# Instruction order in four stages of a decoder layer: start, retention, convolution, passage to the feed-forward part

## The chip, the cores and the metric

The kernel runs on one core of a Trainium2 chip. A core has TensorE (PE, matmul), VectorE (DVE), ScalarE (ACT), GpSimd (POOL) and queues that issue transfers (SyncE, SP, most of them); each engine works through its own queue in order. The metric is device time of one execution in microseconds, the median of the runs.

## The reference

One decoder layer on x of 2048 x 1024 float32, batch 1. A vector c gives shift, scale and gate for two sub-layers (adaLN). The mixing sub-layer puts h = x (1 + scale) + shift through one input projection; its columns feed a gated short convolution and a retention with four heads in chunks of 128. Both results are put through one output projection, then comes a layer norm of alpha x + gate * mix, and then a SwiGLU feed-forward part of width 2816 with a second norm.

```python
mod = sc @ ada_w[layer] + ada_b[layer]
h = x * (1.0 + scale_m) + shift_m
mix = _hybrid_mixer(h, w_in[layer], conv_w[layer], w_out[layer])
x = _layernorm(DN_ALPHA * x + gate_m * mix, ln1_g[layer], ln1_b[layer])
h = x * (1.0 + scale_f) + shift_f
ff = _swiglu(h, w_gate[layer], w_up[layer], w_down[layer])
x = _layernorm(DN_ALPHA * x + gate_f * ff, ln2_g[layer], ln2_b[layer])
...
scores = jnp.einsum('bnihd,bnjhd->bhnij', qc, kc) * decay_mask[None, :, None]
intra = jnp.einsum('bhnij,bnjhe->bnihe', scores, vc)
...
y_conv = _short_conv_mixer(cg, xin, bg, conv_w)
```

## The kernel before

**Numbers.** A float32 matrix is scaled by a power of two from its largest absolute value and split into a high and a low float16 part. A product takes three matmuls (mm3, lines 135 to 137: high x high, high x low, low x high). The high part is made by ScalarE (line 130, or a plain copy), the low part by VectorE (line 131, or a subtraction). The convolution's and the feed-forward's products use seven products in place of eight, with sums and differences of the blocks ahead of and behind them: differences of weights (S1 to S4) and of inputs (T1 to T4), and sums of results (p1, u2, e5). Each of the seven is 4 x 3 = 12 matmuls of 128x512.

**Memory.** Tiles of 128x2048 float32 are "pages" (pg), 24 in all, which are freed and taken by hand. Results of TensorE lie in two pools of four banks, "mm" and "ax", which rotate: the fifth product of a pool waits until the first one's bank has been read.

**Order.** The kernel is written as one sequence of calls. At build time a scheduler with a timeline simulation turns it into one queue for each engine; the order of calls and marks such as `tc.issue_after(x)` (the instructions in the block stand behind x, on x's engine) decide what it may do.

**Stages.** *Start*: input rows, first weights and adaLN sums; `start_bound` bounds the largest h (lines 286, 87, 291), `ret_half_max` takes a weight maximum (line 87). *Retention*, sixteen tiles t of 128 rows: `gemm_ret(t, u)` makes q, k, v and the gate (u = 0 to 3, 24 matmuls each) and evicts them (lines 705 by VectorE, 709 and 711 by ScalarE); `rotary` (734 to 736), `ret_scores` with its masking on VectorE (767), `ret_kv` (782), and for the tile before `ret_y` (793, 796), its norm (800 to 810) and its splits. In between `ret_h(p)` and `ret_hsplit(p)` modulate the rows of a later pair of tiles (line 296, ScalarE) and split them; `h_again` does so once more for the convolution's input. *Convolution*, twelve units: `conv_pair(u, b)` for u = 0 to 5 and both halves b of the sequence, with the seven products in the order 0, 5, 4, 1, 6, 3, 2. `cw_split(u)` scales a unit's weights (880), makes their differences on GpSimd (881 to 884) and both parts of all of them (888 ScalarE, 889 VectorE). `ada_sum` (199) sums modulation weights as they arrive. *Output projection*: pairs of tiles j in the order 0, 1, 4, 5, 6, 7, 2, 3, counted by i. `op_half(t, g)` adds one half of the projection to y (1307), `norm1` is the norm (1267 to 1278, its scaling 1278 by ScalarE), `h2_pair(j)` makes the feed-forward input and its differences (1341 to 1355), `h2_turn(j)` transposes it by transfers (1374). *Passage*: with i = 7 the first feed-forward weights are split: `gu_split1(q)` A11, A12, S1, A22 (1412, 1413), `gu_split2(q)` S2 to S4 (1421 to 1423 the differences, 1426, 1427 the parts). `gu(q, bl)` is one block of the feed-forward's first half for half bl of the sequence. Then come 22 weight blocks q, and the second half. The blocks from about 935 us on are the same before and after.

In `gu` the order of the products and of the sums that free their banks stands as written:

```python
prod(pa, "A11", B11, True, True)
nc.scalar.activation(p1, pa, AF.Copy)
prod(pb, "S2", T2, True, True)
...
prod(pc, "S1", T1_, True, True)
...
prod(pa, "A12", B21, False, True)
...
prod(pd, "A22", T4, True, True)
```

Of the kernel before, what the change touches and what calls it, by code (L numbers as in the profile page):

```python
# [11 lines left out]
F16 = mybir.dt.float16  # L12
# [28 lines left out]
def kernel(ctx: ExitStack, tc: tile.TileContext, xT, x, c, adaN, adaT, ada_b, w_ret, w_conv,  # L41
                             conv_w, w_out, ln1, ln1c, w_gu, w_dn, ln2, rope, consts, out):
    nc = tc.nc
# [531 lines left out]
    with in_order():  # L575
# [75 lines left out]
        ret_half_max(0, 1)  # L651
        start_bound(1, 0)
        start_bound(1, 1)
        start_all(2, 0, (1,))
# [34 lines left out]
    T1 = {}  # L689

    def gemm_ret(t, u):
# [16 lines left out]
        elif u != 3:  # L708
            nc.scalar.activation(dst, ps, AF.Copy, scale=iv)
        else:  # L710
            nc.scalar.activation(dst, ps, AF.Silu, scale=iv)
# [158 lines left out]

    def cw_split(u):
# [12 lines left out]
        nc.gpsimd.tensor_sub(sv[:, 2], f[:, 2], sv[:, 1])  # L884
        cw_views(u)
# [64 lines left out]
    def conv_pair(u, b, done=lambda m: None):  # L950
# [24 lines left out]
        nc.scalar.activation(e5, pc, AF.Copy, scale=iv)  # L975
        prod(pa, 1, False, True)
        prod(pb, 6, False, True)
        nc.vector.scalar_tensor_tensor(p1, pb, iv, p1, op0=OP.mult, op1=OP.add)
        nc.gpsimd.tensor_add(e5, e5, p1)
        pd = new()  # L980
        prod(pd, 3, True, True)
# [94 lines left out]
    for t in range(4, NT):  # L1076
# [22 lines left out]
        if end:  # L1099
            free(*ret_pages[2:4])  # L1100
            cw_split(0)
            cw_max(1)
            hp_load(0, 0)
            hp_load(0, 5)
# [13 lines left out]
        if end:  # L1118
# [3 lines left out]
            hp_load(0, 6)  # L1122
        if t % 2 == 0 and p < 8:
            ret_h(p)
            ret_hsplit(p)
# [3 lines left out]
        if end:  # L1129
            free(*ret_pages[6:8])  # L1130
            hp_load(0, 3)
# [3 lines left out]
        if t in AGAIN:  # L1135
            h_again(AGAIN.index(t))
        elif chores:
            chores.pop()()
# [32 lines left out]
    ahead = [0, 5, 4, 1, 6, 3, 2]  # L1171
    for b in range(2):
        for u in range(6):
# [41 lines left out]
            conv_pair(u, b, done)  # L1215
# [58 lines left out]
    def norm1(y):  # L1274
# [3 lines left out]
        nc.scalar.activation(y, y, AF.Identity, scale=rs, bias=nm)  # L1278
# [50 lines left out]
    def h2_pair(j, tp=None):  # L1329
# [4 lines left out]
        fp = yp[j] if tp else page()  # L1334
# [8 lines left out]
        if tp:  # L1343
            t = [tp[:, i * 512:(i + 1) * 512] for i in range(3)]
# [64 lines left out]
    def gu_split1(q):  # L1409
# [5 lines left out]
        gu_w[q] = {"A11": av[:, :, 0], "A12": av[:, :, 1], "S1": av[:, :, 2], "A22": av[:, :, 3], "pages": [wa]}  # L1415

    def gu_split2(q, eng):
        pg = gu_stage.pop(q)
# [10 lines left out]
        w = gu_w[q]  # L1429
# [8 lines left out]
    u32, ucount, gu_last, gu_pe = [], [0], [None], [None]  # L1438
# [3 lines left out]
    def gu(q, bl, between=None):  # L1442
# [20 lines left out]
        nc.scalar.activation(p1, pa, AF.Copy)  # L1463
        prod(pb, "S2", T2, True, True)
        nc.vector.tensor_add(u2, pb, p1)
# [5 lines left out]
        nc.scalar.activation(u[:, 0], pa, AF.Silu, scale=iv_g)  # L1471
        pd = new()
        prod(pd, "A22", T4, True, True)
        prod(pb, "S3", T3, False, True)
# [4 lines left out]
        prod(pc, "S4", B22, False, True)  # L1479
# [420 lines left out]
```

## Time and profile before

| | us |
|---|---|
| median of 3 runs | 2106.2 (2104.92 to 2108.79) |
| profiled execution | 2106.87 |
| its span | 2104.7 |
| TensorE busy in the span | 2023.1 (96%) |
| VectorE, ScalarE, GpSimd busy | 1463.8, 666.9, 904.9 |
| transfers | 361.06 MB, mean 172 GB/s |

Stage borders on TensorE in us of the span: start to 186, retention to 461, convolution to 790, output projection to 875, passage to 935, then the feed-forward's two halves. The clock is the share of full speed that was granted to TensorE. A row's "idle before" is the time in which the engine stood ahead of the instruction, with the instruction that released it.

### The profile page before, as it was taken

Reading aid. Unit: us, or ns where it says so; the run is one execution under the profiler, and the core shown is the slowest. Engines: PE = TensorE matmul, PEld = TensorE weight load, DVE = VectorE, ACT = ScalarE, POOL = GpSimd, SP = SyncE. Lnnn points to the kernel's source line nnn. Section 1 sums busy time; section 2 is a strip of 40 time slices with the busy share of each in tenths; the row PEclk is TensorE's granted clock in tenths of the full one; section 3 lists DMA queues with packets and bytes.
Section 4 is the critical chain, followed back from the end, with each engine's and each line's share of the span. In section 5 each row is a group of like instructions: output and inputs, shape, how many; then the busy total and the mean of one; then the engine's idle time right before and its main releaser. Section 6 shows DMA issues by size and latency. Waiting matters only on the chain.

```text
span 2104.7 us, 24640 instructions
## 1 busy us (share of the span) xinstructions
PE 2023.1 (96%) x9631; PEld 948.0 (45%) x9631; DVE 1463.8 (70%) x1793; ACT 666.9 (32%) x728; POOL 904.9 (43%) x751
## 2 busy tenths in 40 slices
PE   8899998989899999789999999999999999999998
PEld 3354554444344544334444444444444444444443
DVE  7898846567686577766678768877777354478564
ACT  5523443433422223332323223343433222212210
POOL 3554855555642377742323114544444143134232
PEclk9999999999999999999999999999999999999999
DMA  9048544576873298742444553434343665375321
GB/s 380 26 135 260 163 133 110 161 236 212 269 307 125 85 251 195 186 128 71 149 170 166 184 189 126 160 126 154 131 150 120 237 263 198 139 272 190 150 77 74
DMA packets 189492, 361.06 MB, mean 172 GB/s; under 512 B 118080, under 2 KB 118080, under 8 KB 166592
## 3 DMA queue, kind: packets, MB, share of 16 engines
q1 hardware_dynamic: 181168, 344.55, 49.1%
q10 hardware_dynamic: 8208, 14.95, 2.1%
q8 instruction: 75, 1.23, 0.2%
q14 instruction: 41, 0.34, 0.0%
HBM read 231.26 MB, written 100.93 MB: 158 GB/s over the span
## 4 chain that ended last, share of the span: by engine, by line
PE 42%; DVE 8%; POOL 5%; DMA 5%; issue 2%; ACT 2%; SPq 0%; POOLq 0%; DVEq 0%; ACTq 0%
PE mm L135 7%; PE mm L136 7%; PE mm L137 7%; PE ax L135 7%; PE ax L137 7%; PE ax L136 7%; DMA pg<-yscr 2%; DMA pg<-in_w_dn_dram 2%; POOL pg L1342 1%; DVE pg L1617 1%; ACT pg L1278 1%; DVE wdm L87 1%; DVE pg L1618 1%; DVE pg L1482 1%; POOL rs L1270 1%
## 5 line engine op out<-in xcount | busy, mean ns | idle before, releaser
L135 PE MATMUL mm<-pg,pg 128*128 128x512 f16 x1604 | 609.4, 382 | 18.4 <-ACT pg L1426 8.2
L136 PE MATMUL mm<-pg,pg 128*128 128x512 f16 x1604 | 611.2, 381 | 0.0
L137 PE MATMUL mm<-pg,pg 128*128 128x512 f16 x1604 | 609.5, 381 | 1.7 <-DVE pg L889 1.7
L135 PE MATMUL ax<-pg,pg 128*128 128x512 f16 x1220 | 462.9, 380 | 9.3 <-DVE t2k L973 3.8
L137 PE MATMUL ax<-pg,pg 128*128 128x512 f16 x1220 | 462.6, 380 | 1.5 <-DVE pg L889 1.5
L136 PE MATMUL ax<-pg,pg 128*128 128x512 f16 x1220 | 463.3, 380 | 0.0
L136 PEld LDWEIGHTS <-pg 128*128 128x128 f16 x2888 | 283.3, 98 | 350.4 <-issue 23.7
L135 PEld LDWEIGHTS <-pg 128*128 128x128 f16 x2888 | 283.3, 98 | 345.7 <-issue 9.5
L137 PEld LDWEIGHTS <-pg 128*128 128x128 f16 x2888 | 283.1, 98 | 340.7 <-issue 6.4
L1476 POOL TENSOR_TENSOR pg<-pg,t2k 128x512 f32<-128x512 f32 x44 | 57.9, 1315 | 383.2 <-DVE t2k L1475 207.6
L131 DVE SCALAR_TENSOR_TENSOR pg<-pg,p2s,pg 128x2048 f16<-128x2048 f32 (+1 forms) x42 | 95.9, 2294 | 134.5 <-ACT pg L130 134.4
L130 ACT ACTIVATE pg<-pg,p2s 128x2048 f16<-128x2048 f32 (+1 forms) x42 | 77.6, 1858 | 262.2 <-PE mm L136 114.1
L87 DVE TENSOR_REDUCE m<-pg 128x2 bf16<-128x2048 f32 (+1 forms) x38 | 86.3, 2275 | 20.9 <-DMA pg<-in_w_gu_dram 10.8
L525 PE MATMUL mm<-pg,pg 128*128 128x512 f16 x384 | 89.1, 387 | 5.6 <-DVE pg L533 2.5
L1481 ACT ACTIVATE pg<-t2k,ivg 128x512 f32<-128x512 f32 x44 | 31.6, 717 | 178.1 <-DVE t2k L1480 178.1
L1530 DVE TENSOR_TENSOR pg<-pg,pg 128x2048 f16<-128x2048 f32 (+1 forms) x22 | 46.3, 2103 | 44.6 <-ACT pg L1529 44.6
L1413 DVE TENSOR_TENSOR pg<-pg,pg 128x2048 f16<-128x2048 f32 x22 | 51.7, 2349 | 31.7 <-ACT pg L1412 31.7
L1529 ACT ACTIVATE pg<-pg 128x2048 f16<-128x2048 f32 (+1 forms) x22 | 37.3, 1697 | 99.6 <-DMA wscr<-pg 57.8
L131 DVE SCALAR_TENSOR_TENSOR pg<-pg,hs,pg 128x1024 f16<-128x1024 f32 x32 | 49.4, 1547 | 26.8 <-ACT pg L130 26.6
L1270 POOL TENSOR_SCALAR rs<-mv 128x1 f32<-128x1 f32 x32 | 30.5, 957 | 82.2 <-DVE mv L1268 79.6
L1583 POOL TENSOR_TENSOR pg<-pg,pg 128x2048 f32<-128x2048 f32 (+1 forms) x6 | 26.9, 4491 | 82.0 <-DVE pg L131 38.6
L525 PEld LDWEIGHTS <-pg 128*128 128x128 f16 x384 | 37.5, 99 | 52.4 <-issue 7.7
(278 smaller groups left out, 2782.7 us busy)
## 6 DMA issues: line engine op xcount, KB each, us to landing
pg<-wscr SPq DMA_DIRECT2D x28, 1024.0 KB, 4.8
pg<-in_w_gu_dram SPq DMA_DIRECT2D x22, 1024.0 KB, 4.9
uscr<-pg SPq DMA_DIRECT2D x44, 512.0 KB, 2.8
pg<-in_w_dn_dram SPq DMA_DIRECT2D x22, 1024.0 KB, 5.9
pg<-in_adaT_dram SPq DMA_DIRECT2D x21, 1024.0 KB, 8.2
wscr<-pg SPq DMA_DIRECT2D x77, 256.0 KB, 2.9
yscr<-pg SPq DMA_DIRECT2D x16, 1024.0 KB, 4.3
pg<-uscr SPq DMA_DIRECT2D x16, 1024.0 KB, 5.7
```

The lines of the kernel that those rows point to most:

```text
L87: return nc.vector.tensor_reduce(dst, src, axis=AX.X, op=OP.max, apply_absolute_value=True).ins
L130: nc.scalar.activation(hi, src, AF.Copy, scale=s)
L131: nc.vector.scalar_tensor_tensor(lo, src, s, hi, op0=OP.mult, op1=OP.subtract)
L135: nc.tensor.matmul(ps, l_hi, r_hi, start=start, stop=False, skip_group_check=again)
L136: nc.tensor.matmul(ps, l_hi, r_lo, start=False, stop=False, skip_group_check=again)
L137: return nc.tensor.matmul(ps, l_lo, r_hi, start=False, stop=stop, skip_group_check=again).ins
L525: nc.tensor.matmul(ps, hv[:, a, k, o], w[:, k], start=n == 0 and k == k0, stop=n == 2 and k == k1 - 1)
L1270: nc.gpsimd.tensor_scalar(rs, mv[:, 1:2], EPS / (ALPHA * ALPHA), None, op0=OP.add)
L1413: nc.vector.tensor_sub(wa[:, 2048:], pg, wa[:, :2048])
L1476: nc.gpsimd.tensor_add(e5, e5, p1)
L1529: nc.scalar.activation(o[:, :n, 0], src, AF.Copy)
L1530: nc.vector.tensor_sub(o[:, :n, 1], src, o[:, :n, 0])
```

## The change

- Start: the two bounds of the second pair of rows stand ahead of the weight maximum.
- Retention: `ret_h` and `ret_hsplit` of a later pair are issued behind the ScalarE eviction of u = 2, `h_again` and other small jobs behind that of u = 3. Two loads of the convolution's input change places.
- Convolution: `cw_split` keeps scaling and differences; the parts and their stores are a new function `cw_finish`, called for unit u + 1 in the middle of unit u, behind the eviction of product 4 (e5). Product 3 goes ahead of product 6. 
- Passage: the differences of the first two weight blocks are made on VectorE. With i = 7 both second halves of the projection come first, then `gu_split2(1)`, then the norms, whose scaling is kept back until `gu`'s A12 activation. The first two blocks run `late`: S2 and S4 go behind A22. `gu(0, 1)` stands ahead of `gu_split1(1)`. The last pair's `h2_pair` writes into another page, where before it wrote into y in place behind y's store. Two weight scalings are issued behind a product.

The code, with unchanged lines cut:

```diff
         start_mod(1)
-        ret_half_max(0, 1)
         start_bound(1, 0)
         start_bound(1, 1)
+        ret_half_max(0, 1)
         start_all(2, 0, (1,))
...
     T1 = {}
+    evicted = [None]
...
         elif u != 3:
-            nc.scalar.activation(dst, ps, AF.Copy, scale=iv)
+            evicted[0] = nc.scalar.activation(dst, ps, AF.Copy, scale=iv).ins
         else:
-            nc.scalar.activation(dst, ps, AF.Silu, scale=iv)
+            evicted[0] = nc.scalar.activation(dst, ps, AF.Silu, scale=iv).ins
...
+    cw_parts = {}
...
         nc.gpsimd.tensor_sub(sv[:, 2], f[:, 2], sv[:, 1])
+        cw_parts[u] = (pg, f, sv)
+    def cw_finish(u):
+        pg, f, sv = cw_parts.pop(u)
         cw_views(u)
...
-    def conv_pair(u, b, done=lambda m: None):
+    def conv_pair(u, b, done=lambda m: None, between=None):
         w = cw[u]
...
         prod(pc, 4, True, True)
-        nc.scalar.activation(e5, pc, AF.Copy, scale=iv)
+        read = nc.scalar.activation(e5, pc, AF.Copy, scale=iv).ins
+        if between:
+            with tc.issue_after(read):
+                between()
         prod(pa, 1, False, True)
+        pd = new()
+        prod(pd, 3, True, True)
         prod(pb, 6, False, True)
...
         nc.gpsimd.tensor_add(e5, e5, p1)
-        pd = new()
-        prod(pd, 3, True, True)
         nc.vector.scalar_tensor_tensor(p1, pd, iv, p1, op0=OP.mult, op1=OP.add)
...
             cw_split(0)
+            cw_finish(0)
             cw_max(1)
...
             hp_load(0, 1)
-            hp_load(0, 6)
+            hp_load(0, 3)
         if t % 2 == 0 and p < 8:
-            ret_h(p)
-            ret_hsplit(p)
+            with tc.issue_after(evicted[0]):
+                ret_h(p)
+                ret_hsplit(p)
         if t == NT - 2:
...
             free(*ret_pages[6:8])
-            hp_load(0, 3)
+            hp_load(0, 6)
             hp_load(0, 2)
...
             ret_mix(2)
-        if t in AGAIN:
-            h_again(AGAIN.index(t))
-        elif chores:
-            chores.pop()()
+        with tc.issue_after(evicted[0]):
+            if t in AGAIN:
+                h_again(AGAIN.index(t))
+            elif chores:
+                chores.pop()()
         if t % 2 == 1:
...
-    ahead = [0, 5, 4, 1, 6, 3, 2]
+    ahead = [0, 5, 4, 1, 3, 6, 2]
     for b in range(2):
...
                 free(spp)
-            conv_pair(u, b, done)
+            conv_pair(u, b, done, (lambda u=u: cw_finish(u + 1)) if n < 5 else None)
             if n == 0:
...
         nc.gpsimd.tensor_scalar(nm, mean, rs, -1.0, op0=OP.mult, op1=OP.mult)
-        nc.scalar.activation(y, y, AF.Identity, scale=rs, bias=nm)
+        def scaled():
+            nc.scalar.activation(y, y, AF.Identity, scale=rs, bias=nm)
+        return scaled
...
             hlv.extend(pg.rearrange("p (s a n) -> p s a n", s=4, a=2) for pg in hl)
-        fp = yp[j] if tp else page()
+        fp = tp or page()
         f = fp.rearrange("p (s n) -> p s n", s=4)
...
         if tp:
-            t = [tp[:, i * 512:(i + 1) * 512] for i in range(3)]
+            t = [owner[id(hl[1])][1][:, 1536:2048], yp[j][:, :512], yp[j][:, 512:1024]]
         else:
...
         av = wa.rearrange("p (a s k n) -> p a s k n", a=2, s=4, k=4)
-        gu_w[q] = {"A11": av[:, :, 0], "A12": av[:, :, 1], "S1": av[:, :, 2], "A22": av[:, :, 3], "pages": [wa]}
+        w = gu_w.setdefault(q, {"pages": []})
+        w.update({"A11": av[:, :, 0], "A12": av[:, :, 1], "S1": av[:, :, 2], "A22": av[:, :, 3]})
+        w["pages"].insert(0, wa)
     def gu_split2(q, eng):
-        pg = gu_stage.pop(q)
+        pg = gu_stage[q]
         a = pg.rearrange("p (s n) -> p s n", s=4)
...
         bv = ws[:, :3072].rearrange("p (a s k n) -> p a s k n", a=2, s=3, k=4)
-        w = gu_w[q]
+        w = gu_w.setdefault(q, {"pages": []})
         w.update({"S2": bv[:, :, 0], "S3": bv[:, :, 1], "S4": bv[:, :, 2], "tmp": owner[id(ws)][1][:, 1536:2048]})
...
-    u32, ucount, gu_last, gu_pe = [], [0], [None], [None]
+    u32, ucount, gu_last, gu_pe, gu_act = [], [0], [None], [None], [None, None]
     uscr = [[dram.tile([2, P, NCH, 512], F32, name=f"uscr{b}{r}") for r in range(2)] for b in range(2)]
...
-    def gu(q, bl, between=None):
+    def gu(q, bl, between=None, late=False):
...
         prod(pa, "A11", B11, True, True)
-        nc.scalar.activation(p1, pa, AF.Copy)
-        prod(pb, "S2", T2, True, True)
-        nc.vector.tensor_add(u2, pb, p1)
+        gu_act[0] = nc.scalar.activation(p1, pa, AF.Copy).ins
+        if not late:
+            prod(pb, "S2", T2, True, True)
+            nc.vector.tensor_add(u2, pb, p1)
         prod(pc, "S1", T1_, True, True)
...
         prod(pa, "A12", B21, False, True)
-        nc.scalar.activation(u[:, 0], pa, AF.Silu, scale=iv_g)
+        gu_act[1] = nc.scalar.activation(u[:, 0], pa, AF.Silu, scale=iv_g).ins
         pd = new()
         prod(pd, "A22", T4, True, True)
+        if late:
+            prod(pb, "S2", T2, True, True)
+            nc.vector.tensor_add(u2, pb, p1)
+            prod(pc, "S4", B22, False, True)
+            nc.vector.tensor_add(u2, pc, u2)
         prod(pb, "S3", T3, False, True)
...
         nc.vector.scalar_tensor_tensor(u[:, 0], p1, iv_u, u[:, 0], op0=OP.mult, op1=OP.mult)
-        prod(pc, "S4", B22, False, True)
-        nc.vector.tensor_add(u2, pc, u2)
+        if not late:
+            prod(pc, "S4", B22, False, True)
+            nc.vector.tensor_add(u2, pc, u2)
         nc.scalar.activation(u[:, 1], u2, AF.Silu, scale=iv_g)
...
     order = (0, 1, 4, 5, 6, 7, 2, 3)
+    last_rows = []
     for i, j in enumerate(order):
...
             gu_pages[1].append(page(F16, at=-1))
-            gu_split2(0, nc.gpsimd)
+            gu_split2(0, nc.vector)
+            for t in (2 * j, 2 * j + 1):
+                op_half(t, 1)
+            free(*wo_pages[2:])
+            for n in range(2):
+                gu_pages[n].append(page(F16, at=-1))
+            gu_split2(1, nc.vector)
         for t in (2 * j, 2 * j + 1):
...
                 op_half(t, 0)
-            op_half(t, 1)
-            norm1(ytile(t))
+                op_half(t, 1)
+            scaled = norm1(ytile(t))
+            if i < 7:
+                scaled()
+            else:
+                last_rows.append(scaled)
         if j % 2 == 1:
...
                 h2_turn(j)
-        else:
-            y_store(j)
         if i == 5:
             gu_load(1)
-    free(*wo_pages[2:])
-    for i in range(2):
-        gu_pages[i].append(page(F16, at=-1))
-    gu_split1(1)
-    gu_split2(1, nc.vector)
+    gu(0, 1, late=True)
+    with tc.issue_after(gu_act[0]):
+        gu_split1(1)
+    with tc.issue_after(gu_act[1]):
+        for scaled in last_rows:
+            scaled()
+    y_store(3)
     free(*gu_pages[2])
     gu_pages[2].clear()
-    gu(0, 1)
     for pl in (B11, T2, T1_, B21, T3, T4, B22):
...
     gu_load(3)
-    gu(1, 1)
+    gu(1, 1, late=True)
     gu(0, 0)
...
     gu_max(2)
-    gu_scale(2)
+    with tc.issue_after(gu_pe[0]):
+        gu_scale(2)
     gu_split1(2)
...
     gu_max(3)
-    gu_scale(3)
+    with tc.issue_after(gu_pe[0]):
+        gu_scale(3)
     gu(1, 0)
...
```

ScalarE's queue in the retention. Before, from the modulation of page pg_91 (a later pair) on; mm_2743, mm_2776 and mm_2825 are the products u = 1, 2, 3 of one tile:

```order
L296 ACTIVATE pg_91<-pg_91,mod,msc 128x256 x8
L130 ACTIVATE pg_97<-pg_90,hs 128x2x512
L709 ACTIVATE pg_87<-mm_2743,iv_2222 128x512
L130 ACTIVATE t2k_2738<-pg_89,s_2733 128x512
L356 DMA hcscr_144<-pg_97 128x1024
L709 ACTIVATE pg_87<-mm_2776,iv_2222 128x512
```

After, the same tile's evictions:

```order
L710 ACTIVATE pg_87<-mm_2743,iv_2222 128x512
L130 ACTIVATE pg_91<-pg_78,hs 128x2x512
L356 DMA hcscr_147<-pg_91 128x1024
L356 DMA hcscr_145<-pg_91 128x1024
L710 ACTIVATE pg_87<-mm_2776,iv_2222 128x512
L130 ACTIVATE pg_91<-pg_78,hs 128x2x512
L130 ACTIVATE t2k_2738<-pg_89,s_2733 128x512
L356 DMA hcscr_146<-pg_91 128x1024
L356 DMA hcscr_143<-pg_91 128x1024
L712 ACTIVATE pg_87<-mm_2825,iv_2222 128x512
L296 ACTIVATE pg_90<-pg_90,mod,msc 128x256 x8
```

Modulations now stand behind the eviction of u = 3 (712) or of u = 2 (710). That of pg_91 has moved to the next tile, behind its u = 2.

VectorE's queue around the fourth and fifth unit of the convolution, where the modulation weights are summed (199). Before:

```order
L889 TENSOR_TENSOR pg_86<-pg_76,pg_86 128x4x512
L889 TENSOR_TENSOR pg_79<-pg_78,pg_79 128x3x512
L978 SCALAR_TENSOR_TENSOR t2k_4350<-mm_4348,ivc,t2k_4350 128x512
L982 SCALAR_TENSOR_TENSOR t2k_4350<-mm_4417,ivc,t2k_4350 128x512
L984 SCALAR_TENSOR_TENSOR t2k_4351<-mm_4349,ivc,t2k_4351 128x512
L999 SCALAR_TENSOR_TENSOR pg_85<-mm_4347,ivc,t2k_4351 128x4x128
L199 SCALAR_TENSOR_TENSOR pg_76,mod<-pg_76,pg_75 128x1024 x2
L1004 SCALAR_TENSOR_TENSOR pg_81<-pg_85,convw,pg_81 128x1024
L973 SCALAR_TENSOR_TENSOR t2k_4468<-ax_4465,ivc,t2k_4467 128x512
```

After, the same load's sums (pg_76) and the lo parts of unit 5 (896, in pg_79 and pg_81):

```order
L1009 SCALAR_TENSOR_TENSOR pg_85<-ax_4212,ivc,t2k_4216 128x4x128
L199 SCALAR_TENSOR_TENSOR pg_76,mod<-pg_76,pg_75 128x1024 x2
L104 TENSOR_REDUCE g_4324<-ax_4325 128x1
L1014 SCALAR_TENSOR_TENSOR pg_86<-pg_85,convw,pg_86 128x1024
L114 TENSOR_SCALAR e_4328<-g_4324 128x1
L980 SCALAR_TENSOR_TENSOR t2k_4345<-mm_4342,ivc,t2k_4344 128x512
L1015 SCALAR_TENSOR_TENSOR pg_86<-pg_85,convw,pg_86 128x1024
L116 TENSOR_SCALAR e_4328<-e_4328 128x1
L117 TENSOR_SCALAR s_4323<-e_4328 128x1
L896 TENSOR_TENSOR pg_79<-pg_82,pg_79 128x4x512
L990 SCALAR_TENSOR_TENSOR t2k_4344<-mm_4342,ivc,t2k_4344 128x512
L896 TENSOR_TENSOR pg_81<-pg_78,pg_81 128x3x512
```

The parts stand now between two sums of a unit (980 and 990 are 973 and 978 of before), behind the sums on the load, and a unit earlier than their use.

VectorE's queue at the end of the output projection; 1307 and 1323 add a projected tile to y (mm and ax tiles are its banks), 1352 and 1368 are low parts of the feed-forward input, 1427 and 1445 that of S2 to S4. Before:

```order
L1307 SCALAR_TENSOR_TENSOR pg_79<-mm_6702,io_6635,pg_79 128x512
L1267 BN_STATS st_6730<-pg_79 128x6
L1352 TENSOR_TENSOR pg_92<-pg_97,pg_92 128x4x512
L1355 TENSOR_TENSOR pg_91<-t2k_6601,pg_91 128x512
L1307 SCALAR_TENSOR_TENSOR pg_79<-ax_6716,io_6635,pg_79 128x512
L1427 TENSOR_TENSOR pg_89<-pg_96,pg_89 128x1536
L1307 SCALAR_TENSOR_TENSOR pg_79<-mm_6741,io_6666,pg_79 128x512
```

After:

```order
L1371 TENSOR_TENSOR pg_91<-t2k_6600,pg_91 128x512
L1323 SCALAR_TENSOR_TENSOR pg_81<-mm_6702,io_6635,pg_81 128x512
L1368 TENSOR_TENSOR pg_92<-pg_97,pg_92 128x4x512
L1280 BN_STATS st_6763<-pg_81 128x6
L1445 TENSOR_TENSOR pg_89<-pg_96,pg_89 128x1536
L1323 SCALAR_TENSOR_TENSOR pg_81<-ax_6716,io_6635,pg_81 128x512
L1371 TENSOR_TENSOR pg_91<-t2k_6601,pg_91 128x512
L1371 TENSOR_TENSOR pg_91<-t2k_6602,pg_91 128x512
L1323 SCALAR_TENSOR_TENSOR pg_81<-mm_6730,io_6666,pg_81 128x512
```

The differences of the weights (1421 to 1423, after: 1439 to 1441) stand ahead of these rows now, and two low parts ahead of the last tile of the mm pool, where before one tile of y was read between them.

## Rows read from the trace of the kernel before

**Rows 1.** Stages: us, busy us (instructions) of PE, PEld, DVE, ACT, POOL, PEclk, DMA share, GB/s
```profile
186.00:461.00 275.00, 253.67 (x1322) 135.55 (x1321) 180.64 (x327) 109.84 (x160) 156.48 (x141) 0.95 0.54 158
...
875.00:935.00 60.00, 46.44 (x196) 19.73 (x197) 41.12 (x42) 19.61 (x22) 27.03 (x21) 0.91 0.70 183
...
1400.00:2104.00 704.00, 696.42 (x3238) 315.69 (x3235) 437.50 (x394) 179.12 (x150) 249.44 (x143) 1.00 0.45 164
```

**Rows 2.** What TensorE waited for, 240 to 461: us, times, longest
```profile
PE ax L793 <- DVE pg L767: 12.1, 5, 4.3
PE ax L793 <- DVE g L125: 2.8, 1, 2.8
```

**Rows 3.** What TensorE waited for, 461 to 790
```profile
PE ax L135 <- DVE t2k L973: 3.8, 1, 3.8
...
PE mm L135 <- ACT t2k L971: 0.9, 1, 0.9
PE mm L135 <- DVE t2k L973: 0.9, 1, 0.9
```

**Rows 4.** What TensorE waited for, 870 to 935
```profile
PE mm L135 <- ACT pg L1426: 8.2, 1, 8.2
PE mm L135 <- issue: 2.8, 1, 2.8
PE ax L135 <- ACT t2k L1463: 1.9, 1, 1.9
PE mm L135 <- DMA pg<-pg: 1.0, 1, 1.0
```

**Rows 5.** Stretches of 10 us, columns as in rows 1
```profile
439.00:449.00 10.00, 10.00 (x48) 6.04 (x49) 4.84 (x17) 1.22 (x2) 4.86 (x5) 0.83 0.80 216
577.00:587.00 10.00, 8.31 (x32) 3.51 (x32) 7.28 (x10) 0.00 (x0) 3.01 (x4) 0.83 1.01 428
```

**Rows 6.** Timeline of the start: start us, us, engine line operation [idle before]
```profile
55.81 2.28 DVE L87 TENSOR_REDUCE m<-pg 128x1 bf16<-128x2048 f32 x1
...
58.60 0.29 PE L99 MATMUL ax<-ident,mh 128*128 128x128 f16 x1 [5.53 <-DVE mh L291]
...
64.57 0.69 ACT L530 ACTIVATE pg<-mm,ivs 128x512 f32<-128x512 f32 x1 [2.35 <-PE mm L525]
...
69.58 2.75 PE L525 MATMUL mm<-pg,pg 128*128 128x512 f16 x12 [0.50 <-DVE pg L448]
```

**Rows 7.** Timeline of the retention around the masked scores at 352.21
```profile
340.29 1.13 DVE L810 SCALAR_TENSOR_TENSOR pg<-ax,mv,pg 128x128 f32<-128x128 f32 x4 [9.28 <-POOL pg L807]
...
340.75 4.04 ACT L296 ACTIVATE pg<-pg,mod,msc 128x256 f32<-128x256 f32 x8 [11.12 <-DMA pg<-in_xT_dram]
...
345.87 1.28 DVE L131 SCALAR_TENSOR_TENSOR pg<-pg,hs,pg 128x1024 f16<-128x1024 f32 x1 [3.17 <-ACT pg L130]
...
352.21 0.74 DVE L767 SCALAR_TENSOR_TENSOR pg<-ax,pg,mask 128x512 f32<-128x512 f32 x1
```

**Rows 8.** Timeline of VectorE in the convolution, ahead of the long wait
```profile
561.55 4.42 DVE L889 TENSOR_TENSOR pg<-pg,pg 128x2048 f16<-128x2048 f32 x2 [2.06 <-ACT pg L888]
...
574.40 1.23 DVE L199 SCALAR_TENSOR_TENSOR pg<-pg,pg 128x1024 f32<-128x1024 f32 x1 [4.13 <-DMA pg<-in_adaT_dram]
...
577.89 0.74 DVE L973 SCALAR_TENSOR_TENSOR t2k<-ax,ivc,t2k 128x512 f32<-128x512 f32 x1
```

**Rows 9.** Timeline of VectorE and GpSimd in the passage
```profile
877.48 2.63 DVE L1352 TENSOR_TENSOR pg<-pg,pg 128x2048 f16<-128x2048 f32 x1 [1.71 <-ACT pg L1351]
...
877.92 3.31 POOL L1423 TENSOR_TENSOR pg<-pg,pg 128x512 f32<-128x512 f32 x1
...
884.45 0.74 DVE L1307 SCALAR_TENSOR_TENSOR pg<-mm,io,pg 128x512 f32<-128x512 f32 x1
...
886.30 0.69 DVE L1421 TENSOR_TENSOR pg<-pg 128x512 f32<-128x512 f32 x1
...
903.04 4.64 DVE L1341 TENSOR_TENSOR pg<-pg,pg 128x512 f32<-128x512 f32 x4 [4.42 <-DMA yscr<-pg]
```

## The prediction

> **What bounds the kernel now.** I read the table of stages first. In it TensorE is busy for 696.42 of 704 us of the last stretch, at a granted clock of 1.00, but for 253.67 of 275 us in the retention stretch and 46.44 of 60 us in the passage to the feed-forward part, at 0.95 and 0.91 [rows 1]. So TensorE sets the end, its matmuls follow one another without a break nearly everywhere, and the change can only win back the places where it stands. It adds and removes no matmul. The second view is the list of what TensorE waited for. In the retention it is one thing: the product of the masked scores (line 793) waits for VectorE's masking (line 767), 12.1 us in five waits, and 2.8 us in one more behind a small VectorE step in the same chain [rows 2]. In the convolution the longest wait is 3.8 us for VectorE's u2 sum (line 973), and two more of 0.9 us come at the same products [rows 3]. In the passage it is 8.2 us for the high parts of S2 to S4 (line 1426), and then 1.9, 1.0 and 2.8 us [rows 4].
>
> The third view is the clock. The 10 us after the last wait of the retention and those around the 3.8 us wait show 0.83 granted [rows 5]. With two levels, 1.2 and 2.4 GHz, 0.83 is a third of the time at the lower one: (1 - 0.83) / 0.5 x 10 = 3.4 us, in which half the matmuls are lost, 1.7 us. I add 1.7 us to each wait of some 2.5 us or more that goes, and nothing to shorter ones.
>
> **Start.** Two bounds, of three VectorE operations each, go ahead of the weight maximum (line 87, 2.28 us at 55.81), so the bounds that end TensorE's 5.53 us wait at 58.60 come 2.2 us sooner [rows 6]. The sum of VectorE's work to the next stop does not change. TensorE stands again at 69.58, for a low part (line 448) behind ScalarE's queue [rows 6], and what was won waits there. The only thing that moves out of that chain's way is one ScalarE eviction, 0.69 us at 64.57 [rows 6]. Bounds: nothing and 2.2 us. I take 0.6.
>
> **Retention.** ScalarE has one queue. Before, the modulation of the next rows (line 296, eight operations, 4.04 us) and its high half stood ahead of an eviction of the current rows; the low half (line 131) came at 345.87 after an idle 3.17 us, rotary followed, and the masked scores were reached only at 352.21 [rows 7]. After, these evictions come first, and the modulation of the same page a tile later, behind five of them (first pair of order pieces). In VectorE's queue the masking (line 767, after: 768) of seven tiles in a row stands 1 to 11 rows earlier than before, since fewer of the next rows' splits are ahead of it. I follow two waits to their end, the 4.3 and the 2.8 us one: without 3.17 us of idle and the 1.28 us split ahead, the masking at 352.21 comes at about 348 to 349, and a wait of 4.3 us ends at 353, so some 0 to 0.3 us of it stay. With the clock that is 4.3 + 1.7 + 2.8 + 1.7 = 10.5 us. The other four (7.8 us) have the same shape, but I have not followed their chains to an end: nothing from them. Bounds: 3 us, if the second one stays and the first is halved, to 18 us, if all but the last go with their clock. I take 10.5. The price is in the same queue: eight modulations and four splits start one eviction later, and the input product of the next pair needs them. A tile has four products of 24 matmuls, at 704 us / 3238 = 0.217 us each [rows 1] some 21 us, before they are read, against 4.04 us of modulation and about as much of splits, so this is hidden unless two tiles fall together.
>
> **Convolution.** The weights' parts (lines 888 and 889) leave the spot ahead of a unit's first sums for the middle of the unit before, where VectorE has sums of 0.74 us. Two lo parts, 4.42 us together, stood ahead of them at 561.55; the unit that then waits 3.8 us does so behind a 4.13 us VectorE idle for the modulation weights' load, then two sums of it (1.23 us each) and a tap of the convolution, and only at 577.89 behind them all the u2 sum [rows 8]. After, the sum stands earlier relative to the load, and product 3 gives it 12 matmuls of room. This takes 3.8 + 1.7, and the two 0.9 us waits, 7.3 us. One new wait: VectorE's queue now has the lo parts of unit 5 behind the load's two sums (second order piece), so a late load delays weights and not only one sum. I price it 1.1 us, worked out from the first rows: a 2.2 us lo part, half covered by the product in hand. Net 6.2. Bounds: 2 and 9 us (the upper one with the first waits on line 889 too).
>
> **Passage.** Four things change. The three differences for S2 to S4 go from GpSimd to VectorE: the last of them took 3.31 us on GpSimd at 877.92 and a like one 0.69 on VectorE at 886.30 [rows 9]. The weights are then ready before the last output tiles, so the 8.2 us wait for line 1426 goes. But A22 now comes after A11 and S1 and ahead of A12, and its bank is the last output tile's. VectorE reads that tile last of the third order piece, behind a 2.63 us low part that has to wait for ScalarE, the low part of S2 to S4, another tile and two more low parts: 877.48 + 2.63 and some 4 us, about 884, against 884.45 before [rows 9]. TensorE would finish S1 (12 matmuls, 2.6 us, which it does sooner) and stand again. So of 8.2 us only some 1.5 are won, and the clock falls as before. Bounds: -2 (the eviction later than 885) and 5 us.
>
> The second half is larger. The last pair's products waited 4.42 us until 903.04 for the store of y, since they wrote into y in place [rows 9]. They now write another page, and the norm's scaling stands behind an activation, not ahead of four. The chain behind it, which ends in the transposes for which TensorE stood at the end, comes sooner by those 4.42 us and by the scaling that no longer stands behind the differences of the weights, some 8 us as an estimate, while the matmuls that cover it stay. It had to come 5.7 us sooner: so 1.9 + 1.0 + 2.8 us go [rows 4], with 1.7 us of clock: 7.4. Bounds: 0 (the deferred scaling as late as the old store) and 8. Together 9 us; bounds -2 and 13.
>
> On moving work between GpSimd and VectorE, the rows show that VectorE's low part with two SBUF operands took 2.63 us beside the 3.31 us difference, and a 128x512 difference with GpSimd idle 0.69 [rows 9]. The Trainium skill (SBUF — State Buffer, Who interferes with whom) says that a VectorE instruction with two SBUF inputs and a GpSimd instruction that reads SBUF exclude each other for a whole instruction. By it the first of the three VectorE differences can wait for the GpSimd instruction that runs beside it, an estimate of up to 3.31 us from that row. By that rule the gain in the passage is 5.7 us and not 9, inside its bounds.
>
> **Sum.** 0.6 + 10.5 + 6.2 + 9 = 26.3 us. From the profiled execution's 2106.87 us (span 2104.7, 2.2 outside it) that is 2080.6. The median of the three runs is 0.7 us below the profiled one, so 2080.
>
> **Rivals.**
> - *The waits come back later.* A TensorE that runs ahead reaches the next hi/lo chain sooner: the start shows it, where 2.2 us turn into 0.6. If the second retention wait, the convolution's and the passage's bank do so, 3 + 2 + 4 us are left, and the time is 2097. For it: the convolution has several waits under 1.5 us besides the long one [rows 3], so other chains end close behind. Against: VectorE is idle for 94 of 275 us of that stretch [rows 1], so there is room.
> - *Everything goes.* All six waits of the retention but the last, all of the convolution's and the passage's with their clock: 2.2 + 18 + 9 + 13 = 42 us, 2064. For it: one mechanism, behind-the-eviction order, holds for all six.
> - *The load of the modulation weights takes over (slower).* In the convolution VectorE stands 4.13 us for that load [rows 8] with five of its sums ahead. Now the lo parts of later units stand behind it. If each of five units is late by a lo pair, 4.4 us, and its clock of 1.7, 5 x 6.1 = 30 us are lost against the 26 gained, so 2110. It decides from about four late units on. Against: the long idle for the load shows at one unit, and the splits have some 18 us of a unit (7 products of 12 matmuls) to be done.
> - *Nothing moves* (within 0.2%, 4.2 us: about what runs of this kernel can tell from no change). The retention's and the passage's gains each fall to their lower bound: 3 + 2 - 2 = 3 us, 2104.
>
> **Chances.** The forecast 0.48, everything goes 0.12, waits come back 0.25, nothing moves 0.08, slower 0.07. Faster by over 0.2% is the first three, 0.85; same 0.08; slower 0.07. The range that leaves out 2 in 10 goes from 2064, the sum of the upper bounds, to 2098, just past the case where waits come back.
>
> **What would show it.** The start: the wait near 58.6 is 3.3 us and the stop at 69.6 is longer. Retention: no wait above 2 us between 240 and 420 us; if ScalarE's modulation shows as the releaser of an input product, the price was too low. Convolution: no wait on the u2 sum; a wait on line 896, the lo part's twin, in unit 5 of about 1 us. Passage: a wait of 6 us or so for A22's bank, released by line 1323, and no wait for transposes. From 1400 us on both traces must be alike; any difference there says that something other than waits has changed. The prediction is wrong if the retention keeps waits of over 2 us, or TensorE's busy time and clock change outside those four places.

## The result, and the profile after

The changed kernel takes 2095.12 us in the median of 4 runs (2092.47 to 2097.59), the one before 2106.53 (2104.92 to 2108.79, 4 runs): a ratio of 0.9945, 95% interval [0.9928, 0.9962]. It is faster by 11.4 us, where the forecast was 26 (the stated range was 2064 to 2098 us). The profiled execution has a span of 2095.8 us, at a mean granted clock of 0.991.

Where the difference arises is read best by a count of matmuls. Both kernels issue the same 9631; the start of the n-th in the trace before less that in the trace after is how far the changed kernel is ahead there. (In the retention and the convolution the order of matmuls differs a little between the two, so the borders are places where it is the same work again. The border at 2300 lies at 493 us, so that row holds the first unit of the convolution too.) In us:

| stage, matmuls | forecast | measured |
|---|---|---|
| start, to 700 | 0.6 | 0.6 |
| retention, to 2300 | 10.5 | -0.9 |
| convolution, to 3300 | 6.2 | 2.8 |
| output projection, to 4050 | 0 | -1.3 |
| passage, to 4300 | 9.0 | 9.2 |
| feed-forward part, to the end | 0 | -1.2 |

The rows add up to 9.2 us, which is what these two traces differ by; the medians differ by 11.4. The last row is not the change's: traces of further kernels with the same feed-forward code show -0.7 to -4.1 there against this one trace of before. The other rows scatter as well. Kernels with the changed code in a stage give -1.4 to 0.6 at the start, 1.9 to 5.8 in the convolution and 8.8 to 9.3 in the passage; the retention is -0.9 in a second trace of the changed kernel (e13 below) and 2.3 in e7, whose instructions stand in the same order there. So a row is to be read with 2 to 3 us of doubt, the passage's with less than 1.

The table of stages of the changed kernel, over the stretches of [rows 1], the last one to this kernel's own end (us, then busy us and instructions of PE, PEld, DVE, ACT, POOL, then clock, DMA share, GB/s):

```profile
186.00:461.00 275.00, 248.74 (x1326) 134.65 (x1323) 176.87 (x327) 113.96 (x165) 156.37 (x141) 0.96 0.55 159
...
875.00:935.00 60.00, 53.48 (x241) 23.47 (x240) 43.00 (x45) 19.24 (x23) 24.83 (x19) 0.97 0.69 176
1400.00:2095.00 695.00, 687.18 (x3193) 311.64 (x3191) 427.89 (x385) 174.52 (x146) 249.71 (x140) 1.00 0.45 164
```

The passage has gained 45 matmuls in its 60 us and the granted clock has risen from 0.91 to 0.97. In the retention TensorE does 4 matmuls more in 275 us, which is next to nothing. What it waited for there, in the changed kernel (us in total, times, longest; the answer to [rows 2]):

```profile
PE ax L135 <- DMA pg<-pg: 9.9, 3, 5.0
PE ax L99 <- DVE m L87: 6.7, 1, 6.7
PE ax L136 <- DMA pg<-pg: 1.8, 1, 1.8
PE ax L794 <- DVE g L123: 1.5, 1, 1.5
PE mm L135 <- ACT pg L710: 0.6, 1, 0.6
```

The waits for the masking (line 768 is 767 of before) are gone, as the prediction said; one of 1.5 us in the same chain is left. But the list adds up to 20.5 us, where before it was 17.0 (the 14.9 of [rows 2] and four kinds of small ones). Four are scores (lines 135 and 136, ax) that wait for transposes of q and k, 11.7 us; one is a weight maximum. Follow the longest, at 347.22, back through the queues:

```profile
318.81 1.41 DVE L131 SCALAR_TENSOR_TENSOR pg<-pg,pg,pg 128x512 f16<-128x512 f32 x2 [2.77 <-ACT pg L130]
...
341.18 1.28 DVE L131 SCALAR_TENSOR_TENSOR pg<-pg,hs,pg 128x1024 f16<-128x1024 f32 x1
...
342.50 3.66 SPq L754 DMA_TRANSPOSE pg<-pg  x2
...
347.22 0.27 PE L135 MATMUL ax<-pg 128*128 128x128 f16 x1 [4.96 <-DMA pg<-pg]
```

The transposes' own input, the low parts of rotated q and k in the first row, was ready at 320.2 us. They are issued 0.04 us after a low part of modulated rows ends, at 342.46, and SyncE had issued nothing since 316. That low part reads the page that `ret_transpose` has just taken for its result: `h_again` freed it, as written, one call earlier. In the kernel before the same transposes stand at 329.30, again when the last low part of that page ends:

```profile
326.70 2.57 DVE L131 SCALAR_TENSOR_TENSOR pg<-pg,hs,pg 128x1024 f16<-128x1024 f32 x2
...
329.30 4.46 SPq L753 DMA_TRANSPOSE pg<-pg  x2
...
336.03 0.22 PE L135 MATMUL ax<-pg 128*128 128x128 f16 x1 [0.28 <-DMA pg<-pg]
```

There it was just not in time: the scores waited 0.28 and 0.37 us. The 3.63 us wait at 373.61 has the same form (issued at 367.64, a low part ends at 367.61). The other two, 1.33 and 1.83 us at 281 and 283, do not: their transposes, from 277.62 on, follow their own high and low parts. (A fifth, 2.54 us at 468.41, lies just behind the window; its transposes stand behind another one in SyncE's queue.)

The weight maximum has the same cause. A load of convolution weights goes into a page whose last reader is such a low part:

```profile
426.64 1.53 DVE L131 SCALAR_TENSOR_TENSOR pg<-pg,hs,pg 128x1024 f16<-128x1024 f32 x1
...
428.20 0.33 SPq L859 DMA_DIRECT2D pg<-in_w_conv_dram  x1
...
434.37 2.29 DVE L87 TENSOR_REDUCE m<-pg 128x1 bf16<-128x2048 f32 x1 [1.14 <-DMA pg<-in_w_conv_dram]
...
436.71 0.29 PE L99 MATMUL ax<-ident,m 128*128 128x128 f16 x1 [6.74 <-DVE m L87]
```

The waits grew by more than the stage lost. Between matmuls 700 and 2300 TensorE waits 24.0 us before and 30.4 after, but the stretches at the lower granted clock (1.2 GHz) there fall from 27.3 to 20.5 us, where a matmul of 512 columns comes every 0.43 us instead of every 0.22 (from 349.09 us, for one), so that half of that time is lost. So 3.4 of the 6.4 us came back through the clock; the rest was not traced.

In the convolution the waits of [rows 3] on the u2 sum are gone, one of 0.89 us for ScalarE's copy (978, before: 971) is left, and one of 2.17 us is new, for a small VectorE chain (the second modulation's bound):

```profile
612.88 5.64 POOL L465 TENSOR_TENSOR pg<-pg,pg 128x1024 f32<-128x1024 f32 x2
...
616.24 3.37 DVE L199 SCALAR_TENSOR_TENSOR pg<-pg,pg 128x1024 f32<-128x1024 f32 x1
...
619.53 1.22 DVE L199 SCALAR_TENSOR_TENSOR pg<-pg,pg 128x1024 f32<-128x1024 f32 x1
...
622.61 0.75 DVE L990 SCALAR_TENSOR_TENSOR t2k<-ax,ivc,t2k 128x512 f32<-128x512 f32 x1
...
623.41 0.27 PE L99 MATMUL ax<-ident,m 128*128 128x128 f16 x2 [2.17 <-DVE t2k L990]
```

In the passage, after [rows 4], these stand (TensorE, idle before):

```profile
878.91 0.38 PE L135 MATMUL mm<-pg,pg 128*128 128x512 f16 x1 [0.75 <-ACT t2k L1482]
...
884.05 0.38 PE L135 MATMUL mm<-pg,pg 128*128 128x512 f16 x1 [1.96 <-DVE pg L1323]
...
889.69 0.38 PE L135 MATMUL mm<-pg,pg 128*128 128x512 f16 x1 [2.90 <-ACT pg L1487]
```

The 8.2, 1.9, 1.0 and 2.8 us of before have become 0.75, 1.96 and 2.90, and two under 0.8 behind them. A bank wait came as forecast, but S2 met it and not A22, and it took 1.96 us: the 24 matmuls of A22 and A12 lie ahead of it.

### The profile page after: what moved, and what is told of

Same layout as the page of the kernel before. It is cut to its first block, busy times and chain, and to the rows that moved or that the text cites. A ratio compares the mean times of both kernels' runs of the same rounds, so it can differ in the third digit from the quotient of the medians.

```text
span 2095.8 us, 24601 instructions
## 1 busy us (share of the span) xinstructions
PE 2016.2 (96%) x9631; PEld 947.0 (45%) x9631; DVE 1460.0 (70%) x1796; ACT 666.6 (32%) x728; POOL 903.6 (43%) x748
## 4 chain that ended last, share of the span: by engine, by line
PE 45%; DVE 6%; DMA 4%; POOL 2%; issue 1%; ACT 1%; SPq 0%; POOLq 0%; DVEq 0%; ACTq 0%
PE ax L135 8%; PE ax L137 8%; PE ax L136 8%; PE mm L135 7%; PE mm L137 7%; PE mm L136 7%; DMA pg<-in_w_dn_dram 2%; DMA pg<-yscr 1%; DVE wdm L87 1%; DVE pg L1643 1%; DVE pg L1445 1%; DVE pg L1508 1%; DVE pg L1644 1%; POOL pg L1501 0%; DVE pg L1503 0%
```

## The experiments

Theory A after the result: the marks keep the modulated rows' work back, that work frees its pages later, and the transposes and loads that go into those pages are late by as much as the masking gains. Rival B of e1 to e4: the marks win their 10 us, and the other parts, joined to them, cost it again. Ratios are against runs of the kernel before on the same chip, with 95% intervals. The stage figures are counts of matmuls as above.

**e1 and e2: the marks alone, and everything but the marks.** e1 is the kernel before with `evicted[0]` and the two marks; e2 is the changed kernel with

```diff
-            with tc.issue_after(evicted[0]):
-                ret_h(p)
-                ret_hsplit(p)
+            ret_h(p)
+            ret_hsplit(p)
...
-        with tc.issue_after(evicted[0]):
-            if t in AGAIN:
-                h_again(AGAIN.index(t))
+        if t in AGAIN:
+            h_again(AGAIN.index(t))
```

> The kernel before with the retention's two marks alone (modulation and splits issued behind an eviction). Theory A (the marks take away TensorE's waits for the masked scores, but hold the pages of the modulated rows longer; the transposes of q and k and the loads of convolution weights go into those pages and come late): waits on line 793's twin fall below 3 us between 240 and 461 us, 8 to 15 us of waits for transposes and for a weight maximum come in their place, 2104 to 2108 us. Rival B (the marks win their 10 us and the convolution's and passage's parts, joined to them, cost it again): no new wait for transposes, 2094 to 2098 us.

> The changed kernel without the retention's two marks; start, convolution and passage as changed. Theory A: waits for the masked scores come back (some 12 to 15 us between 240 and 461), the waits for transposes (9.9 + 1.8 us) and for the weight maximum (6.7 us) go; 2091 to 2095 us, that is no slower than the changed kernel. Rival B: the retention's gain is missing, 2100 to 2106 us. Rival C (the transposes are late because the transfers themselves are slower in the changed kernel): the waits for transposes stay.

e1: 0.9984 [0.9971, 0.9997], 2106.57 us against 2108.82; retention 1.5 us. What TensorE waited for from 240 to 461 us:

```profile
PE ax L135 <- DMA pg<-pg: 9.3, 3, 5.1
PE ax L99 <- DVE m L87: 7.1, 1, 7.1
PE ax L136 <- DMA pg<-pg: 1.9, 1, 1.9
```

e2: 0.9945 [0.9929, 0.9961], as the changed kernel; retention -0.3. Its 2097.84 us lie above the 2091 to 2095 that were expected, on a chip where the kernel before takes 2108.82. There the masking is back:

```profile
PE ax L794 <- DVE pg L768: 13.2, 5, 4.3
PE ax L135 <- issue: 1.2, 1, 1.2
PE ax L794 <- DVE g L125: 1.1, 1, 1.1
PE ax L136 <- DMA pg<-pg: 1.0, 2, 0.7
```

The exchange is made by the two marks alone, and the rest of the change neither causes nor cures it. Rival B falls, and so does rival C of e2, slow transfers: the waits for transposes are down to 1.0 us, or 2.2 with the one that the list calls issue.

**e3 and e4: one mark each.** e3 drops the mark on `h_again`, e4 the one on `ret_h` and `ret_hsplit`.

> The changed kernel without the mark on h_again (the convolution's input once more), with the one on ret_h and ret_hsplit. Theory A, as h_again's x page is the one that the next transposes write: the waits for transposes fall from 11.7 to under 5 us, 2088 to 2094 us. Rival B: as the changed kernel, 2094 to 2097 us.

> The changed kernel without the mark on ret_h and ret_hsplit, with the one on h_again. Theory A: the waits for transposes at about 347 and 373 us stay (5.0 and 3.6 us), 2094 to 2098 us. Rival B: as the changed kernel or up to 5 us slower, with waits for the masked scores back.

e3: 0.9932 [0.9913, 0.9951], retention 3.4 us; the waits for transposes fall from 11.7 to 2.1 us, as expected, and the weight maximum's is gone. But 6.1, 4.2 and 2.4 us come for VectorE (lines 123, 706, 125), which now has that work ahead of the tile's own, and the 2095.30 us miss the 2088 to 2094 expected. e4: 0.994 [0.9924, 0.9956], retention -1.9; transposes 10.0 us in all, though at 288, 347 and 450 us where 347 and 373 were expected, and 4.8 us more ahead of scores that the list calls issue. So it is `h_again`'s mark that holds the pages.

**e5 and e6: convolution and passage alone.**

> The kernel before with the convolution's part alone (cw_finish behind the e5 eviction, product 3 ahead of 6). Prediction's term: 6.2 us between 461 and 790. Theory A (the 3.8 us wait and the two of 0.9 go with 1.7 us of clock, 7 us, but a new wait on a small VectorE chain at some 620 us costs 4): 3 us, 2103 on the chip of the first runs. Rival B (the new wait at 620 us comes only from the joined parts): 7 us, 2099.

> The kernel before with the passage's part alone. Theory: the stage's gain stands by itself, 8 to 10 us between 870 and 935 us and nothing elsewhere: 2096 to 2098 if the kernel before is 2106 on that chip. Rival: part of it comes from the other stages' order, 4 to 6 us.

e5: 0.9985 [0.9976, 0.9994], 2.4 us in its stage, with the wait at the second modulation's bound:

```profile
PE ax L99 <- DVE t2k L989: 2.5, 1, 2.5
```

So that wait belongs to the part itself. e6: 0.9961 [0.9947, 0.9976], 9.0 us in its stage and 0.5 or less ahead of the projection. Within the doubt the parts add up: 1.5 + 2.4 + 9.0 is 12.9 us of stage gains, against 11.1 for the three joined. The start's part was not run alone.

**e7: the 2.9 us wait in the passage.** ScalarE's queue had the high part of the second block's S2 to S4 (waiting for VectorE's differences) ahead of the eviction that S4's bank waits for. The edit, inside `gu` (the earlier call of `gu_split2(1)` goes):

```diff
-        nc.scalar.activation(e5, pc, AF.Copy)
-        if between:
+        gu_e5 = nc.scalar.activation(e5, pc, AF.Copy).ins
+        if late and between:
+            with tc.issue_after(gu_e5):
+                between()
+        elif between:
...
-            gu_split2(1, nc.vector)
...
-    gu(0, 1, late=True)
+    gu(0, 1, lambda: gu_split2(1, nc.vector), late=True)
```

> The changed kernel with gu_split2(1) behind the e5 eviction of gu(0, 1), where ScalarE's high part of it stood ahead of that eviction and TensorE waited 2.9 us for it (line 1487 at 889.69). Theory: the 2.9 us wait and its 1.7 us of clock go, 3 to 5 us faster than the changed kernel. Rival: the wait for S4 is replaced by the one for its bank or low part, under 1 us faster.

0.9951 [0.9937, 0.9966], passage 8.5 us: no gain. The eviction is in time now, and the next instruction waits for VectorE, whose low parts stand in front of a sum:

```profile
886.78 0.39 PE L137 MATMUL ax<-pg,pg 128*128 128x512 f16 x1 [0.95 <-DVE pg L1429]
...
893.37 0.38 PE L135 MATMUL mm<-pg,pg 128*128 128x512 f16 x1 [3.82 <-DVE t2k L1499]
```

The expectation was wrong: the rival was right.

**e8 to e12: the pages themselves.** e8 calls `h_again` behind the eviction of u = 1 (its old call goes). e9 gives the transposes of tiles from 8 on a buffer that nothing uses until the convolution (the scores read it there). e10 is both, e11 is e3 with that buffer, e12 is the kernel before with it.

```diff
+        if t in AGAIN:
+            with tc.issue_after(evicted[0]):
+                h_again(AGAIN.index(t))
         gemm_ret(t, 2)
...
-        dst = T1[t].bitcast(F16)[:, :2048]
+        dst = (gfrow if t > 7 else T1[t]).bitcast(F16)[:, :2048]
```

> The changed kernel with h_again one product earlier, behind the eviction of u = 1 and no longer behind u = 3. Theory A (page release): the x page is free one product (5.3 us) or more sooner, so the waits for transposes fall from 11.7 to 0 to 5 us while the waits for masked scores stay below 4 us: 3 to 8 us faster than the changed kernel. Rival B (VectorE's own work is what is late, wherever it stands): the waits come back as waits for masking or for line 706, total between 240 and 461 us within 3 us of the changed kernel's 20.5.

> The changed kernel with the transposes of q and k, for tiles from 8 on, written into a buffer that is not in use until the convolution (gfrow), and no longer into a page just freed by h_again. Nothing else differs in the code. Theory A (page release): the waits for transposes between 240 and 461 us fall from 11.7 to under 4 us, and the retention then shows part of the forecast gain; 2087 to 2093 us where the changed kernel has 2095. Rival B (VectorE is late anyhow): the same time turns up as waits for the masked scores or a norm, 2093 to 2097. Rival C (the transfers are slow): waits for transposes stay.

> Both: transposes into their own buffer, and h_again behind the eviction of u = 1. Theory A: the 3.1 us wait for a transpose that was left with the earlier h_again goes, 2 to 5 us faster than with it alone (0.9928 of before), 0.991. Rival B: within 0.1% of it.

> Transposes into their own buffer, and no mark on h_again. Theory A: with no mark the page was free in time already (2.1 us of waits for transposes), so within 2 us of the run without the mark (0.9932 of before). Rival B: the same. If it is faster by more than 3 us, pages were still the limit there.

> The kernel before with transposes into their own buffer. Theory A: before the change the order of VectorE's queue, not the pages, held the masked scores: within 3 us of before (0.9985 to 1.0005). Rival D (pages were the limit before the change as well): 6 us or more faster, and the waits for the masked scores shrink.

Waits of TensorE from 240 to 461 us; in brackets the part of the others that belongs to the convolution's first weights (lines 895 and 896):

| | ratio | retention, us | transposes | weight maximum | others |
|---|---|---|---|---|---|
| changed | 0.9945 [0.9928, 0.9962] | -0.9 | 11.7 | 6.7 | 2.1 |
| e8 | 0.9928 [0.9911, 0.9944] | 5.5 | 3.6 | 0 | 14.8 (6.0) |
| e9 | 0.9936 [0.9921, 0.9951] | 2.1 | 1.8 | 7.1 | 8.0 (2.9) |
| e10 | 0.9902 [0.9885, 0.9919] | 11.7 | 0.3 | 0 | 11.9 (2.6) |
| e11 | 0.9957 [0.9941, 0.9973] | -1.4 | 0 | 0 | 18.0 |
| e12 | 1.0002 [0.9992, 1.0011] | -1.6 | 0 | 0 | 20.1 (1.7) |

The brackets matter for the comparison: in the changed kernel these waits stand at 461.41 and 464.34 (1.82 and 0.60 us), just behind the window, and a kernel that is ahead meets them inside it.

e9's edit changes where the transposes write, and it settles what held them:

```profile
320.10 2.61 SPq L754 DMA_TRANSPOSE gfrow<-pg  x2
...
342.64 2.32 DVE L131 SCALAR_TENSOR_TENSOR pg<-pg,hs,pg 128x1024 f16<-128x1024 f32 x1 [0.19 <-ACT pg L130]
```

The same transposes are issued from 320.10 on, as their inputs get ready, 25 us before the low part ends that had held them. Up to 333 us VectorE's queue has the same order in both traces. Their waits go from 11.7 to 1.8 us, and the 1.8 is the wait at 283 that was no matter of a page. But the time, 2094.81 us, did not reach the 2087 to 2093 expected of it; it lies where rival B put it. Some 3 us more come back as other waits, the weight maximum stays at 7.1 (SyncE's load still stood 15.4 us behind a low part), and from 333 us on the build puts VectorE's queue in another order, so this time is not that of the buffer alone.

e8 alone takes the maximum's wait and most of the transposes'. Its 18.4 us of waits in all, against 20.5, are what rival B allowed, and 6.1 us of masking is more than theory A did; but 6.0 of the 18.4 are the convolution's first weights, and the count gives the retention 6.4 us more than in the changed kernel. With the buffer and the earlier `h_again` together both kinds are gone: e10. From e8 to e10 VectorE's queue keeps its order through the retention, so this is the cleanest look at the buffer: 5.5 to 11.7 us. The retention then shows about what had been forecast. What it waits for, 240 to 461 us:

```profile
PE ax L794 <- DVE pg L768: 9.3, 2, 4.9
PE mm L137 <- DVE pg L896: 2.3, 1, 2.3
PE mm L135 <- ACT pg L895: 0.3, 1, 0.3
PE ax L135 <- DMA gfrow<-pg: 0.3, 1, 0.3
```

Two masking waits are left: the marks do not do away with all of them, and the 10.5 us were right as an amount more than by the way in which they were counted. Between matmuls 700 and 2300 e10 waits 17.8 us against 24.0 before, and is at the lower clock for 17.1 us against 27.3: 6.2 us of waits and some 5 of clock. e12 shows that room by itself is worth nothing before: there the masked scores still wait for VectorE. e11 missed its expectation. It is 3.8 us above e3 in the medians (of two chips), with waits of 6.6 and 4.6 us for VectorE and one of 5.5 that the list calls issue and that ends 0.1 us behind the masking; why the order without that mark suffers more with the new buffer was not settled.

**e13 and e14: e10 and the changed kernel on one chip.**

> The changed kernel once more, on the chip of e14. By every theory 0.993 to 0.996 of before.

> The kernel of e10 once more beside the changed one. Theory A (pages held by h_again cost the retention's term, and with them free it appears): 5 to 10 us below the changed kernel on the same chip. Rival (the difference between e10 and the changed kernel was one of chips): within 3 us of it.

The changed kernel 0.9935 [0.9922, 0.9947] at 2095.61 us; with both edits 0.9905 [0.9889, 0.992] at 2088.43: 7.2 us below it, and the fastest version found. Stage by stage it is the retention again, 12.7 against -0.9 us, with 9.3 in the passage in both.

## Why the prediction was wrong, point by point

- *Start*, 0.6 us: the mechanism was right. The wait at 58.6 became 3.46 us at 56.46, as forecast, and all but 0.5 us was given back by 69.04. Whether that 0.5 us lasts can't be told from the scatter.
- *Retention*, 10.5 us, measured -0.9: the step that failed. The masking waits went as worked out; that part was right. Wrong was the price. The prediction priced the marks by one thing, that modulation and splits end later, and put this at nothing because their results are read a tile later; the mark on `h_again`, which did the harm, it did not price at all. The results were in time. It was the pages that this work reads which were not: a page is free when its last reader has ended, and 24 pages are all that there are, so the transposes of the next tile (8.6 of the 11.7 us) and a weight load (6.7 us) wait to write into them. The rows that tell it are SyncE's, and no group of the prediction had one; in the trace of before the transposes at 329.30 already stood against the end of a low part, and the scores behind them already waited 0.65 us. The prediction's own sign, no wait above 2 us between 240 and 420 us, failed at 347 and 374.
- *The clock's 1.7 us for each longer wait* is no fixed price: in the 10 us from 373 on, behind a wait of 3.63 us, 1.00 was granted, and 0.83 in those from 623 on, behind one of 2.17.
- *Convolution*, 6.2 us, measured 2.8: the removed waits were right with their clock, but for one of the two of 0.9 us, which was ScalarE's and has a twin after (the changed kernel goes from 1.1 us behind to 6.3 ahead between matmuls 2500 and 2700). The wait priced at 1.1 us for a low part came as 1.54 us at 563.97 for a high part (line 895, ScalarE); before has 1.24 us at that place. Missing was the new wait of 2.17 us at 623.41 with the lower clock after it: the lead falls from 6.3 to 2.5 us between matmuls 2700 and 3000.
- *Passage*, 9 us, measured 9.2: right in sum and mostly in its parts. The bank wait was put at A22 with 6 us; it was 1.96 at S2. The wait of 2.90 us behind it was not foreseen, so the first half still gave about what was said (2.2 us, forecast 1.5), and the second gave 7.0 (forecast 7.4).
- *Rivals*: the likeliest in hindsight was "the waits come back later", 2097. Its total agrees by luck: its 3 + 2 + 4 us are -0.9, 2.8 and 9.2, and in the retention it named a second wait for VectorE, where the runs show page release. No wait of TensorE in the convolution names the load of the modulation weights.
- The output projection's -1.3 us stands in e1, e5 and e12 as well (-2.1, -1.1, -0.9), where nothing there was changed: it is no effect of the change.

## What to carry to other kernels

A mark that holds work back can cost nothing on the engine that it holds back and still make something late elsewhere: list what the held work reads, when those buffers come free, and who writes them next, in the queues that issue transfers too. Where a wait goes and the stage does not move, read what took its place in the list of waits before anything else, and give the new claimant a buffer of its own to see whether it was the buffer. Parts of a joined change are best judged by how far ahead the n-th matmul is, stage by stage; the total hid a 9 us gain and an 11 us miss. Look also at whether a small edit has left the queues in their order: here a new buffer alone reordered VectorE's.

## What the runs showed of the hardware

VectorE's sum on line 199 takes 1.22 us at 619.53, but 3.37 us at 616.24, while two GpSimd additions run from 612.88 to 618.52. It ends 1.1 us after them, as if it had begun then. The Trainium skill (SBUF — State Buffer, Who interferes with whom) has it that a VectorE instruction with two SBUF inputs and a GpSimd instruction that reads SBUF shut each other out; this trace agrees, with 2.15 us lost. The sum stands in VectorE's queue ahead of the chain that ends in the 2.17 us wait, and e5 has the same pair, 3.36 us and a wait of 2.5; that the one makes the other was not tested. In the passage, where that rule had been weighed, the first block's three differences on VectorE took 1.10, 1.10 and 1.75 us beside GpSimd, against 0.69 alone [rows 9], and no wait of TensorE has them as its releaser. The second block's took 0.67 to 0.68 us each; the 2.90 us wait comes behind them through ScalarE's queue.
